# Prompt attention with packed score passes, plain float32 P v in column tiles, and row sums on VectorE and GpSimd

## Chip, core and metric

One core of one Trainium2 chip runs the kernel. The metric is the device time of one execution in microseconds (us). Three runs of the kernel before took 1915.83, 1916.79 and 1921.95 us; the median is 1916.79.

## What is computed

One hybrid decoder layer, for a prompt of 2048 tokens and 8 samples of 8 new tokens. A projection feeds a multi-head latent attention (MLA, 8 heads) and a gated linear attention (GLA, 4 heads); their outputs are gated, projected, and followed by a gated per-token term and a norm. The change lies in the prompt's MLA:

```
s = (einsum('bqhd,bkhd->bhqk', qn_b, k_nope)          # 64 values a head
     + einsum('bqhr,bkr->bhqk', qr_b, k_rope)) * scale  # 32 rotary values, one key for all heads
s = where(kpos <= qpos, s, -inf)
p = softmax(s)
o = einsum('bhqk,bkhd->bqhd', p, v)                   # 64 values a head
```

All of it is float32. TensorE's one-pass type, float32r, holds fewer bits, so the kernel splits operands in two float32r parts, hi + lo, and adds hi\*hi + hi\*lo + lo\*hi in PSUM.

## The kernel before

The work goes in stages: pass A (projections, queries, keys, values, stored to DRAM), pass B (GLA), prompt attention interleaved with the samples' decode attention, and the output projection. A scheduler that plays the program through puts the instructions of each engine in their final order; on each engine they run in that order.

`attention` is a generator. It goes over 32 units (h, j): 8 heads, and for each the query tiles j = 3, 2, 1, 0 of 512 queries. A unit has 4j + 4 key blocks of 128 keys, of which the last four lie on the diagonal and take only 512, 384, 256 and 128 queries (`c0`). For each block `attend` does this:

- three TensorE passes of float32r make the scores, keys on the partitions and queries along the row, in a PSUM tile `psC` of one bank, two in turn (L963 with the hi parts, 64 nope + 32 rope + 1 row for the maximum = 97 contraction rows; L964 and L965 with the lo parts, 96 rows);
- ScalarE takes the exponential twice, rounded (`ph`, L967) and full (`pf`, L969); VectorE makes `pl` = `pf` - `ph` (L971); on the diagonal GpSimd masks both (L974);
- three passes accumulate P v in `poC` (L976, L977, L978). The stationary side holds v's lo, hi and a block of ones, so that the row sums of P come out of the same passes.

Ahead of each unit `maxima` computes its row maxima: one score pass of the hi parts with queries on the partitions (L933) into `pmC`, reduced on VectorE (L935, L938, L940), transposed by L948 and copied by ScalarE into row 96 of the queries. The unit's loop mixes the next unit's maxima between its own blocks, and the main loop runs 0.8 attention steps for each step of `decode` (its TensorE passes are L770 to L833, its GpSimd work L51, L750 to L764). After a unit, `ob` is copied out and stored (L981 to L983).

The SBUF places of head 6's and 7's keys, values and queries are handed on to the output stage (`places`) for its weights; `early` is the place of head 6's values, through which the first weights are staged in three tiles.

Of the kernel before, what the change touches and what calls it, by code (L numbers as in the profile page):

```python
# [41 lines left out]
BASE = 8          # the innermost blocks of the GLA chunk  # L42
FLOOR = -20.0     # least log decay of a step inside them


def emit(ctx, tc, I, O):
# [48 lines left out]
    # hi and lo parts of queries, keys (both transposed) and values  # L95
# [3 lines left out]
    Kr = dram.tile([DR + 1, 2, S], F32, name="Kr")     # last row: ones  # L99
    Vd = dram.tile([NT, P, H, 2, DV], F32, name="Vd")  # L100
# [3 lines left out]
    Dd = dram.tile([H, S], F32, name="Dd")            # sums of P  # L104
    Rd = dram.tile([H, T], F32, name="Rd")            # their reciprocals
# [11 lines left out]
    # sample group, kept for the decode attention  # L117
# [19 lines left out]
    # ------------------------------------------------------------------ pass A: latents, queries, keys, values  # L137
    def pass_a(wb):
        """returns the weights of pass B, which take the place of this pass's as soon as these are done"""
        with ExitStack() as c:  # L140
# [17 lines left out]
            def xload(t0, W, add):  # L158
                """x^T in two parts, and the sums of squares over each partition's rows"""
# [22 lines left out]
            def scales(acc, W, tiles):  # L182
                """1 / rms of the tokens, along the rows (R) and along the columns"""
# [18 lines left out]
            def load_wide(ws, src, g=None, cp=A):  # L202
                """weights of each 128 rows of src, and of all its columns, into [P, hi|lo, columns] of ws"""
# [46 lines left out]
            def latents(z, q, i, m, lat, la, cs):  # L250
# [33 lines left out]
                # forget gate logits, from the low-rank rows and the row of ones  # L284
# [7 lines left out]
            def forget(la, W, t0):  # L292
                """log sigmoid(x) / 16, with log sigmoid(x) = min(x, 0) - ln(1 + exp(-|x|))"""
# [25 lines left out]
            def gates_sample(x, i, m, t0):  # L319
                """few tokens: they are the stationary side, and the result is transposed"""  # L320
# [41 lines left out]
            def keys_values(lat, t0, n):  # L362
# [8 lines left out]
                for q in range(n):  # L371
# [3 lines left out]
                    qq = sp.tile([P, H, 2, DV], F32R, name="qq", bufs=3)  # L375
                    zv = z.rearrange("p (h d) -> p h d", h=H)
                    split(qq[:, :, 1], qq[:, :, 0], zv)
                    nc.sync.dma_start(Vd[t0 // P + q], qq.bitcast(F32))

            for mi, (t0, W, tiles) in enumerate(macros):  # L380
# [29 lines left out]
                else:  # L410
                    # most of the gates last: their operands' places go to the weights of pass B as they are done
# [8 lines left out]
    def weights_b(ww, xp, gm):  # L420
        """in the places of pass A's operands, in the order in which it gives them up"""
# [13 lines left out]
    # ------------------------------------------------------------------ pass B: gated linear attention  # L435
    def pass_b(ws, xp, wb):
        with ExitStack() as c:
# [22 lines left out]
            rst = wp.tile([P, 4, P], F32, name="rst")       # 0 where a cumulation begins, else 1  # L460
# [10 lines left out]
            # second factors [2 heads x 64, pair, head of the pair, token], zero off the diagonal  # L471
# [4 lines left out]
            # state [2 heads x 64, pair, head of the pair, 128], zero off the diagonal  # L476
# [27 lines left out]
            def gla(cnt, i, m, qk, v, gt):  # L504
# [6 lines left out]
                # transposed q, k [2 heads x 64, pair, token] and cumulated log decay  # L511
# [8 lines left out]
                # inside the base blocks a step's log decay is held at -20 (e^-20 is far below a float32's last bit)  # L520
# [23 lines left out]
                # q exp(b), k exp(b_last - b)  # L544
# [13 lines left out]
                # A^T[s, t] by levels: first halves of blocks of 2L against their second halves  # L558
# [59 lines left out]
                # outputs and state  # L618
# [55 lines left out]
                # norm and gate  # L674
# [23 lines left out]
    # ------------------------------------------------------------------ decode attention  # L698
    def decode(c):
        """a generator; each step is a piece of work"""  # L700
# [5 lines left out]
        CK = 8                      # key blocks of 128 in a chunk  # L706
        NCK = 4                     # chunks of a sample
# [15 lines left out]
        # q in the latent space [c, b, hi|lo, h, t], and the rope stack [hi; hi; lo]  # L723
# [12 lines left out]
        qrs = wp.tile([96, NB, 2, H, TD], F32R, name="qrs")    # second half zero: it adds nothing to the lo rows  # L736
# [76 lines left out]
        def fresh(b, mx, dn, oc):  # L813
            """the keys of the new tokens"""
# [74 lines left out]
    # ------------------------------------------------------------------ prompt attention  # L889
    def attention(c, we, slots):  # L890
        """a generator; each step is a block of 128 keys against a tile of 512 queries.
        The places of the keys and values go to slots as they are done."""
# [4 lines left out]
        pS = pool(c, "psC", 2, PSUM, side="right")  # L897
# [5 lines left out]
        VT = [wp.tile([P, NT, 192], F32R, name=f"VT{i}") for i in range(2)]  # L903
        for k in KT:
            for a in range(4):
                nc.sync.dma_start(k[a][DN:97].bitcast(F32), Kr[:, :, a * 512:a * 512 + 512])
        for v in VT:
            gcopy(v[:, :, P:192], ones[:, 0:DV].unsqueeze(1).broadcast_to([P, NT, DV]))

        def load(h):  # L910
            k, v = KT[h % 2], VT[h % 2]
            for a in range(3, -1, -1):
# [367 lines left out]
```

## Time and profile before

| | |
|---|---|
| runs | 1915.83, 1916.79, 1921.95 us |
| profiled execution, first to last instruction | 1922.2 us |
| TensorE matmuls busy in it | 1786.5 us (93%) |
| VectorE, ScalarE, GpSimd busy | 1215.8, 919.9, 687.2 us |
| mean granted TensorE clock | 0.965 |

The profiled execution's span is 0.3% above the median of the runs. A matmul's row gives its shape as contraction rows\*stationary columns, then the moving operand. Matmuls overlap in the pipeline, so the time that a pass costs is read from one start to the next, not from the duration. A plain float32 matmul shows as two rows (x2), since it is carried out in two halves.

### The profile page before, as it was taken

The page shows a single profiled execution, that of the slowest core. Times are in us where ns is not written, and L with a number is a line of the kernel's source. Part 1 is how long each engine was busy: PE and PEld are TensorE (multiplying, and loading weights), DVE is VectorE, ACT ScalarE, POOL GpSimd, SP SyncE. Part 2 cuts the span into 40 slices and gives each one's busy share as a digit, 9 for nine tenths or more (in the row PEclk, how much of TensorE's full clock was granted, in tenths as well). Part 3 has the DMA queues.
Part 4 walks back from the last instruction along what each step waited for, and adds up shares of the span by engine and source line. Part 5 has one row for each costly group of instructions (what it writes and reads, how often), then busy time and mean ns, then how long its engine had stood idle before and what let it go on. Part 6 is the DMA issues. An engine that isn't in the chain of part 4 may idle for free.

```text
span 1922.2 us, 27335 instructions
## 1 busy us (share of the span) xinstructions
PE 1786.5 (93%) x9296; PEld 1427.9 (74%) x9296; DVE 1215.8 (63%) x2640; ACT 919.9 (48%) x2184; POOL 687.2 (36%) x1043
## 2 busy tenths in 40 slices
PE   4999987899999996999999999999998999999997
PEld 3877776688787784677777777777776788888885
DVE  6376466566744766788878888888887433323333
ACT  4354455334332433677776777777783112212112
POOL 5263352343433332544444444454436100000000
PEclk7999999899989997899999999999999999999999
DMA  5164476511111107223323232322217432222211
GB/s 167 42 232 158 147 267 212 136 39 38 48 31 45 45 23 178 68 71 94 83 78 100 58 86 72 97 80 77 79 37 237 120 94 83 88 84 73 77 48 33
DMA packets 150374, 183.74 MB, mean 96 GB/s; under 512 B 18682, under 2 KB 93291, under 8 KB 150235
## 3 DMA queue, kind: packets, MB, share of 16 engines
q1 hardware_dynamic: 144090, 161.02, 27.8%
q0 software_dynamic: 6144, 20.98, 3.6%
q8 instruction: 74, 1.21, 0.3%
q14 instruction: 66, 0.53, 0.1%
HBM read 125.60 MB, written 56.35 MB: 95 GB/s over the span
## 4 chain that ended last, share of the span: by engine, by line
PE 67%; DVE 5%; DMA 4%; ACT 2%; issue 1%; POOL 1%; SPq 0%; POOLq 0%; DVEq 0%; ACTq 0%
PE pgE L63 6%; PE pgE L65 6%; PE pgE L64 6%; PE pgB L65 4%; PE pgB L63 4%; PE pgB L64 4%; PE poC L976 3%; PE poC L978 3%; PE psC L963 3%; PE pmC L933 3%; PE poC L977 3%; PE psC L964 3%; PE psC L965 3%; DVE pl L971 1%; PE poD L803 1%
## 5 line engine op out<-in xcount | busy, mean ns | idle before, releaser
L971 DVE TENSOR_TENSOR pl<-pf,ph 128x512 fp32r<-128x512 f32 (+1 forms) x320 | 230.2, 724 | 42.4 <-ACT pf L969 38.2
L967 ACT ACTIVATE ph<-psC 128x512 fp32r<-128x512 f32 (+1 forms) x320 | 171.0, 534 | 126.2 <-PE psC L965 68.6
L969 ACT ACTIVATE pf<-psC 128x512 f32<-128x512 f32 (+1 forms) x320 | 170.2, 532 | 0.0
L935 DVE TENSOR_REDUCE mxC<-pmC 128x1 f32<-128x512 f32 x192 | 129.6, 682 | 30.4 <-PE pmC L933 28.3
L933 PE MATMUL pmC<-KT,qC 96*128 96x512 f32 (+2 forms) x320 | 122.8, 402 | 20.1 <-DVE mxC L940 6.5
L976 PE MATMUL poC<-ph,VT 128*128 128x512 f32 (+1 forms) x320 | 124.0, 387 | 4.5 <-ACT ob L981 3.0
L978 PE MATMUL poC<-pl,VT 128*128 128x512 f32 (+1 forms) x320 | 122.6, 384 | 2.0 <-DVE pl L971 1.8
L963 PE MATMUL psC<-qC,KT 97*128 97x512 f32 (+1 forms) x320 | 121.8, 381 | 0.5 <-ACT pf L969 0.4
L964 PE MATMUL psC<-qC,KT 96*128 96x512 f32 (+1 forms) x320 | 119.0, 372 | 0.0
L965 PE MATMUL psC<-qC,KT 96*128 96x512 f32 (+1 forms) x320 | 118.6, 371 | 0.0
L977 PE MATMUL poC<-ph,VT 128*64 128x512 f32 (+1 forms) x320 | 117.0, 366 | 0.0
L1146 ACT ACTIVATE thE<-pgE 128x512 f32<-128x512 f32 x32 | 19.1, 598 | 153.6 <-PE pgE L65 153.6
L1147 DVE SCALAR_TENSOR_TENSOR thE<-thE,pgE 128x512 f32<-128x512 f32 x32 | 22.0, 688 | 111.0 <-ACT thE L1146 111.0
L933 PEld LDWEIGHTS pmC<-KT,qC 96*128 96x128 f32 x320 | 62.4, 198 | 37.9 <-DVE mxC L935 10.9
L64 PE MATMUL pgE<-wpg,hh 128*128 128x512 f32 x224 | 87.7, 391 | 0.0
L63 PE MATMUL pgE<-wpg,hh 128*128 128x512 f32 x224 | 87.6, 391 | 0.0
L51 POOL TENSOR_SCALAR chl<-cr 128x1024 fp32r<-128x1024 f32 x32 | 38.3, 1198 | 137.4 <-PE poD L803 137.3
L65 PE MATMUL pgE<-wpg,hl 128*128 128x512 f32 x224 | 85.4, 392 | 0.0
L1150 POOL TENSOR_TENSOR ssE<-ssE 128x1 f32<-128x1 f32 (+1 forms) x17 | 3.3, 195 | 219.9 <-ACT yE L1149 219.9
L1090 POOL TENSOR_TENSOR raw<-raw 128x512 f32<-128x512 f32 (+1 forms) x17 | 22.2, 1308 | 161.5 <-DMA raw<-Rd 161.5
L60 DVE TENSOR_TENSOR x<-x 128x512 fp32r<-128x512 f32 (+2 forms) x74 | 64.5, 917 | 22.3 <-PE pgB L64 14.2
L750 POOL DMA_INDIRECT cr<-in_ckv,idx x32 | 36.7, 1148 | 116.5 <-PE poC L978 53.1
(475 smaller groups left out, 5396.3 us busy)
## 6 DMA issues: line engine op xcount, KB each, us to landing
x<-in_xT SPq DMA_DIRECT2D x32, 512.0 KB
x<-in_w_in SPq DMA_DIRECT2D x16, 512.0 KB
Qn<-qq SPq DMA_DIRECT2D x16, 512.0 KB
Kn<-qq SPq DMA_DIRECT2D x16, 512.0 KB
Vd<-qq SPq DMA_DIRECT2D x16, 512.0 KB
KT<-Kn SPq DMA_DIRECT2D x32, 256.0 KB
VT<-Vd SPq DMA_DIRECT2D x8, 1024.0 KB
qC<-Qn SPq DMA_DIRECT2D x32, 256.0 KB
```

What stands on the lines that cost most here:

```text
L63: T_.matmul(out, ah, bh, start=first, stop=False)
L64: T_.matmul(out, ah, bl, start=False, stop=False)
L65: T_.matmul(out, al, bh, start=False, stop=last)
L933: T_.matmul(ps[:, :w], qs, kv[0][cb][:96, 0, :w], start=True, stop=True)
L963: T_.matmul(ps[:, c0:], kh[:, ks], qh[:, c0:], start=True, stop=False)
L964: T_.matmul(ps[:, c0:], kh[:96, ks], ql[:, c0:], start=False, stop=False)
L965: T_.matmul(ps[:, c0:], kl[:, ks], qh[:96, c0:], start=False, stop=True)
L967: A.activation(ph[:, c0:], ps[:, c0:], AF.Exp, scale=SC)
L971: V.tensor_tensor(pl[:, c0:], pf[:, c0:], ph[:, c0:].bitcast(F32), op=ALU.subtract)
L976: T_.matmul(o[:, c0:], vt[:, kb, DV:192], ph[:, c0:], start=kb == 0, stop=False)
L977: T_.matmul(o[:DV, c0:], vt[:, kb, 0:DV], ph[:, c0:], start=False, stop=False)
L978: T_.matmul(o[:, c0:], vt[:, kb, DV:192], pl[:, c0:], start=False, stop=kb == nk - 1)
```

## The change

- **Scores.** The contraction of hi and lo parts, 3 x 96 rows and the maximum, is laid out in 2.5 passes of 128 rows. Pass 0 (l = 0, L980) holds 64 hi nope rows and the rope keys' hi and lo parts against the rope queries' hi; pass 1 (l = 1) holds nope lo\*hi and hi\*lo. What is left, rope hi against query lo and the row of ones for the maximum, are 33 rows: L983 takes them for an even block from partitions 0 to 32 and for the odd block from 64 to 96, two row tiles of 64. Keys and queries are loaded in more pieces (`load`, `queries`: 9 and 7 DMAs where 5 and 2 were), and pass A no longer splits v.
- **Blocks go in pairs.** One `psC` tile of two banks holds a pair's scores, and there is one such tile where there were two of one bank. Off the diagonal one exponential goes over both banks; its result `p` is plain float32.
- **P v.** L998 multiplies v (64 columns, float32, unsplit) with `p`; even blocks go to PSUM partitions 0 to 63, odd ones to 64 to 127. `ob` adds the halves (a ScalarE copy, a VectorE addition).
- **Sums.** `sum0` and `sum1` collect P along the keys: blocks with kb % 3 = 1 on VectorE, the others on GpSimd (L1007). After a unit L1017 sums over the partitions with a matrix of ones, 8 matmuls in column tiles of 32.
- **Places.** `early` has one staging tile where it had three; the list of places is rearranged.

```diff
-                T_.matmul(ps[:, c0:], kh[:, ks], qh[:, c0:], start=True, stop=False)
-                T_.matmul(ps[:, c0:], kh[:96, ks], ql[:, c0:], start=False, stop=False)
-                T_.matmul(ps[:, c0:], kl[:, ks], qh[:96, c0:], start=False, stop=True)
-                ph = pp.tile([P, 512], F32R, name="ph")
-                A.activation(ph[:, c0:], ps[:, c0:], AF.Exp, scale=SC)
-                pf = pp.tile([P, 512], F32, name="pf")
-                A.activation(pf[:, c0:], ps[:, c0:], AF.Exp, scale=SC)
...
-                T_.matmul(o[:, c0:], vt[:, kb, DV:192], ph[:, c0:], start=kb == 0, stop=False)
-                T_.matmul(o[:DV, c0:], vt[:, kb, 0:DV], ph[:, c0:], start=False, stop=False)
-                T_.matmul(o[:, c0:], vt[:, kb, DV:192], pl[:, c0:], start=False, stop=kb == nk - 1)
+        pS = pool(c, "psC", 1, PSUM, side="right")
...
+            for k0 in range(0, nk, 2):
+                pair = [(kb, kb % 2, max(kb - 4 * j, 0) * P) for kb in (k0, k0 + 1)]
+                ps = pS.tile([P, 2, 512], F32, name="psC")
+                for kb, e, c0 in pair:
+                    ks = slice(kb % 4 * P, kb % 4 * P + P)
+                    for l in range(2):
+                        T_.matmul(ps[:, e, c0:], kt[kb // 4][:, l, ks], q[:, l, c0:], start=l == 0, stop=False)
+                for kb, e, c0 in pair:
+                    rows = slice(64 * e, 64 * e + 33)
+                    T_.matmul(ps[:, e, c0:], K3[rows, kb // 2], q[rows, 2, c0:], start=False, stop=True)
+                yield
+                p = pp.tile([P, 2, 512], F32, name="p")
+                if k0 < 4 * j:
+                    A.activation(p, ps, AF.Exp, scale=SC)
+                else:
+                    for kb, e, c0 in pair:
+                        A.activation(p[:, e, c0:], ps[:, e, c0:], AF.Exp, scale=SC)
+                        G.affine_select(p[:, e, c0:c0 + P], p[:, e, c0:c0 + P], pattern=[[1, P]],
+                                        compare_op=ALU.is_ge, fill=0.0, base=0, channel_multiplier=-1)
...
+                for kb, e, c0 in pair:
+                    T_.matmul(o[64 * e:64 * e + 64, c0:], vt[:, kb], p[:, e, c0:], start=kb < 2, stop=kb >= nk - 2)
+                for kb, e, c0 in pair:
+                    f = kb % 3 == 1
...
+                        (V if f else G).tensor_tensor(sums[f][:, c0:], sums[f][:, c0:], p[:, e, c0:], op=ALU.add)
+                yield
...
+            for e in range(2):
+                for i in range(4):
+                    T_.matmul(sm[32 * i:32 * i + 32, :P], ones[:, :32], sums[e][:, i * P:(i + 1) * P], start=e == 0, stop=e == 1)
```

The built order shows where this puts the instructions. TensorE before, in the middle of the attention; L963 to L965 are a block's scores, L976 to L978 its P v, L933 a pass of the next unit's maxima, L770 to L783 the decode attention:

```order
L963 MATMUL psC<-qC,KT_6778 128x512
L964 MATMUL psC<-qC,KT_6778 128x512
L965 MATMUL psC<-qC,KT_6778 128x512
L781 MATMUL ptD<-cth,qlat 128x512
L782 MATMUL ptD<-ctl,qlat 64x512
L783 MATMUL ptD<-krT,qrs 128x512
L770 MATMUL ptD<-ident,cr 128x128 x4
L963 MATMUL psC<-qC,KT_6778 128x512
L964 MATMUL psC<-qC,KT_6778 128x512
L965 MATMUL psC<-qC,KT_6778 128x512
```

Two blocks' scores can stand there in a row, since there are two tiles for them. TensorE now, with two pairs of blocks off the diagonal (L980 and L983 scores, L998 P v, L949 maxima; the numbers of the decode's lines are lower by two):

```order
L998 MATMUL poC<-p,VT_6766 64x512 x2
L980 MATMUL psC<-qC,KT_6758 128x512 x4
L983 MATMUL psC<-qC,K_6765 128x512 x2
L774 MATMUL ptD<-identr,krs 96x128 x4
L949 MATMUL pmC<-KT_6758,qC 128x512
L779 MATMUL ptD<-cth,qlat 128x512
L780 MATMUL ptD<-ctl,qlat 64x512
L998 MATMUL poC<-p,VT_6766 64x512 x2
```

Each pair's P v follows its scores with maxima and decode work in between, and the next pair's scores follow P v. At a unit's end, on the diagonal, TensorE's order now is:

```order
L998 MATMUL poC<-p,VT_6767 64x512
L774 MATMUL ptD<-identr,krs 96x128 x4
L998 MATMUL poC<-p,VT_6767 64x384
L779 MATMUL ptD<-cth,qlat 128x512
L780 MATMUL ptD<-ctl,qlat 64x512
L980 MATMUL psC<-qC,KT_6761 128x512 x4
L983 MATMUL psC<-qC,K_6765 128x512 x2
L1017 MATMUL pmC<-sum_13379,ones 32x128
L949 MATMUL pmC<-KT_6761,qC 128x128
L998 MATMUL poC<-p,VT_6767 64x256
```

The two P v matmuls of a pair stand apart there, with other passes between them.

More of the change, by code (lines that the diff above doesn't have):

```diff
@@ L923, in maxima @@
+            for l in range(2):
+                nc.sync.dma_start(qf[0:DN, l], Qn[hs, 0, ts])
+            nc.sync.dma_start(qf[DN:P, 1], Qn[hs, 1, ts])
+            for r0 in (64, 96):
+                nc.sync.dma_start(qf[r0:r0 + DR, 0], Qr[rs, 0, ts])
+            for r0 in (0, 64):
+                nc.sync.dma_start(qf[r0:r0 + DR, 2], Qr[rs, 1, ts])
+            return q
         def maxima(j, kv, q):
@@ L948, in maxima @@
                 T_.matmul(mr[0:1, i * P:(i + 1) * P], m4r[:, i:i + 1], identr, start=True, stop=True)
-            A.activation(qh[96:97], mr[0:1], AF.Copy)
+            for r0 in (32, 96):
+                A.activation(q[r0:r0 + 1, 2], mr[0:1], AF.Copy)
             yield
         def attend(h, j, kv, q):
-            (kt, vt), qt = kv, q
-            qh, ql = qt[:, 0], qt[:96, 1]
+            kt, vt = kv
             o = po.tile([P, 512], F32, name="poC")
+            sums = [sp.tile([P, 512], F32, name=f"sum{e}") for e in range(2)]
@@ new lines, in attend @@
+            ob = sp.tile([DV, 512], F32, name="ob")
+            A.activation(ob, o[DV:P], AF.Copy)
+            V.tensor_tensor(ob, ob, o[:DV], op=ALU.add)
+            nc.sync.dma_start(Od[h * DV:(h + 1) * DV, j * 512:j * 512 + 512], ob)
+            sm = pm.tile([P, 512], F32, name="pmC")
+            for e in range(2):
+                for i in range(4):
+                    T_.matmul(sm[32 * i:32 * i + 32, :P], ones[:, :32], sums[e][:, i * P:(i + 1) * P], start=e == 0, stop=e == 1)
+            rc = sp.tile([P, P], F32, name="rcC")
```

110 lines of the change are left out of this document (51 added, 59 removed).

## Prediction

> **What bounds the kernel now.** I read the page's first part, then the windows, to see which engine limits the stage that is changed.
>
> ```profile
> span 1922.2 us, 27335 instructions
> PE 1786.5 (93%) x9296; PEld 1427.9 (74%) x9296; DVE 1215.8 (63%) x2640; ACT 919.9 (48%) x2184; POOL 687.2 (36%) x1043
> ...
> core 0: us, PE busy (x) PEld busy (x) DVE busy (x) ACT busy (x) POOL busy (x), PEclk, DMA share, GB/s
> 900.00:1000.00 100.00, 96.48 (x556) 76.83 (x555) 85.27 (x225) 77.90 (x163) 51.29 (x76) 1.00 0.31 85
> 1100.00:1200.00 100.00, 94.84 (x527) 75.15 (x527) 85.01 (x223) 74.40 (x160) 45.13 (x69) 0.98 0.30 83
> ```
>
> The attention is TensorE's: it is busy 95 to 96 of 100 us, at the full clock. VectorE (85) and ScalarE (75 to 78) are near, GpSimd (45 to 51) is not. The stage's length is in the first and last starts of its maxima and of its last P v pass:
>
> ```profile
> L933 PE MATMUL pmC<-KT,qC x320: 220/394/796, 752.7 to 1434.4; 96*128 96x512 f32 x128, 96*128 96x128 f32 x16, 96*128 96x384 f32 x16
> L978 PE MATMUL poC<-pl,VT x320: 224/394/793, 792.0 to 1459.3; 128*128 128x512 f32 x128, 128*128 128x256 f32 x32
> ```
>
> That is 707 us, 752.7 to 1459.3. So the price of a TensorE pass decides. The timeline gives it from start to start, and the groups by form the number of passes:
>
> ```profile
> 1304.00 0.40 PE L933 MATMUL pmC<-KT,qC 96*128 96x512 f32 x1
> 1304.23 0.40 PE L963 MATMUL psC<-qC,KT 97*128 97x512 f32 x1
> ...
> 1305.18 0.39 PE L976 MATMUL poC<-ph,VT 128*128 128x512 f32 x1
> 1305.41 0.40 PE L977 MATMUL poC<-ph,VT 128*64 128x512 f32 x1
> 1305.64 0.40 PE L963 MATMUL psC<-qC,KT 97*128 97x512 f32 x1
> ...
> L976 PE MATMUL poC<-ph,VT 128*128 128x512 f32 x224 | 94.3, 421 | 4.5 <-ACT ob L981 3.0 <-POOL ph L974 1.4
> L976 PE MATMUL poC<-ph,VT 128*128 128x384 f32 x32 | 11.7, 366 | 0.0
> L976 PE MATMUL poC<-ph,VT 128*128 128x256 f32 x32 | 10.1, 316 | 0.0
> L976 PE MATMUL poC<-ph,VT 128*128 128x128 f32 x32 | 7.8, 243 | 0.0
> ```
>
> A 512-wide pass costs 0.235 us (seven in 1.64). Each kind of pass has 224 x 512 + 32 x (384 + 256 + 128) = 139,264 columns, as much as 272 full passes or 136 full pairs of blocks.
>
> **Packing: what it saves on TensorE.** For plain float32 in tiled modes, pass B has two places to read. In the first, single matmuls (x2 rows) in two different tilings alternate; in the second, four matmuls go to two column tiles in turn, between full-array passes:
>
> ```profile
> 569.66 0.43 PE L657 MATMUL poB<-ident,oi 128*64 128x128 f32 x2
> 570.02 0.43 PE L656 MATMUL poB<-v,AT 64*64 64x128 f32 x2
> 570.38 0.43 PE L657 MATMUL poB<-ident,oi 128*64 128x128 f32 x2
> ...
> 577.19 0.39 PE L63 MATMUL pgB<-wg,x 128*128 128x512 f32 x1
> 577.42 0.39 PE L64 MATMUL pgB<-wg,x 128*128 128x512 f32 x1
> 577.74 0.65 PE L666 MATMUL ptB<-v,km 64*64 64x128 f32 x8
> 578.32 0.50 PE L65 MATMUL pgB<-wg,x 128*128 128x512 f32 x1
> 578.66 0.40 PE L63 MATMUL pgB<-x 128*128 128x512 f32 x1
> ```
>
> Call w a 128-column float32 matmul, s a change of tiling. The first place gives w + s = 0.36. The second gives 0.58 for four matmuls and one change: with two at a time, 2w + s = 0.58. So w = 0.22 and s = 0.14. One at a time, 4w + s = 0.58 would leave w = 0.07, less than one 128-column pass of float32r at full rate for what must be several (0.235 / 4 = 0.06). So column tiles do run together. As a check on s over the whole visit: from 577.42 to 578.66 are 1.24 us, in which two full passes (0.46) and 2w (0.44) account for 0.90; 0.34 is left for going in and out, 0.17 each. I take 0.15 for a change.
>
> A full pair of blocks took 12 passes, 2.82 us. Now it takes five (the two L983 row tiles counted as one), 1.18, and P v with 512 columns at 4w = 0.88, together 2.06. It saves 0.76, and over 136 pairs 104 us. Three things take from that:
>
> - On the diagonal the pair's halves are of unequal width, and the tiles last as long as the wider; and 34 of the 160 pairs have their two L998 apart in the built order (the third piece of order above), so that each pays alone. Added up over the order with w, P v comes to 141 us instead of 136 x 0.88 = 120: 21 lost. L983 loses 2.
> - The sums, L1017: 8 matmuls a unit in four column tiles, 8w / 4 = 0.44, over 32 units 14; many stand apart, so 18.
>
> Net, 104 - 41 = 63 us less work.
>
> **Packing: what it costs.** Counted in the built orders from the first maxima to the last pass of the attention, TensorE changes its tiling 115 times before and 851 times now: full array to row tiles (L983), back to maxima or decode, to column tiles (L998), back again. That is 736 more, at 0.15 us 110 us. The Trainium skill, page "TensorEngine Tiling (Array Packing)", section "Tiling Modes", speaks against the change here: it says that changing the tiling mode, not merely the tile, drains TensorE. The trace agrees where rows or float32 column tiles change (0.14 to 0.17 us), but not for the 64-column float32r pass L977, which stands between full passes at the usual 0.23 us.
>
> Sum for TensorE: -63 + 110 = +47 us.
>
> **The other engines and the waits.** They get lighter or stay covered:
>
> ```profile
> L967 ACT ACTIVATE ph<-psC 128x512 fp32r<-128x512 f32 x224 | 134.1, 599 | 107.0 <-PE psC L965 60.8 <-PE poC L977 26.6 <-PE pmC L933 8.2
> L967 ACT ACTIVATE ph<-psC 128x256 fp32r<-128x256 f32 x32 | 12.3, 385 | 0.8 <-PE psC L965 0.2
> L971 DVE TENSOR_TENSOR pl<-pf,ph 128x512 fp32r<-128x512 f32 x224 | 161.4, 725 | 35.4 <-ACT pf L969 33.3 <-PE poC L978 0.6
> L764 POOL TENSOR_TENSOR chl<-cr,chl 128x1024 fp32r<-128x1024 f32 x32 | 77.7, 2429 | 1.3
> ```
>
> ScalarE: by the two widths an exponential costs 0.17 us and 0.84 ns a column, so 1.03 for two banks where four of 0.60 were: some 185 us less. VectorE loses the subtractions and gains 72 additions of about 0.7 us, copies and reciprocals: some 120 less. GpSimd gains 184 additions; at 2.43 us for 1024 columns a 512-wide one is 1.2, together 220 us, less 64 masks' worth; it goes from about 330 to 520 busy of 750 us. It stays under TensorE.
>
> The new wait is the single `psC` tile: a pair's P v and the next pair's scores both wait for its exponential. From the start of the last score pass that is 0.40 (its duration) + 1.03 + about 0.1, and 1.3 us of it are free for other passes. In the order stand there maxima and decode passes, 1.24 us in the median by the spacings above; what is missing to 1.3 adds up to 31 us over the 160 pairs. Queued behind the waiting L998 are the next scores and the maxima; ScalarE and VectorE wait for those. Against it stand the waits that were named before:
>
> ```profile
> PE pmC L948 <- DVE mxC L927: 7.0, 10, 0.8
> PE pmC L933 <- DVE mxC L940: 6.5, 6, 1.4
> ...
> PE pmC L933 <- DVE mxC L935: 3.3, 6, 1.2
> PE poC L976 <- ACT ob L981: 3.0, 7, 1.0
> ```
>
> About 20 us that lighter engines may end, and as much again, since a pass after a wait starts with an unhidden weight load. I set the two against each other, 0, with -45 and +80 as bounds: everything named gone twice over; or the 31 us paid and another 50 where the diagonal's P v waits for masks that stand behind additions on GpSimd (64 diagonal pairs, up to one 1.2 us addition each, less what is covered).
>
> **Other stages.** Pass A's values lose a split, of which TensorE's wait may give back some:
>
> ```profile
> L63 PE MATMUL pq<-lat,wq 128*128 128x512 f32 x48 | 19.3, 427 | 13.4 <-DVE qq L60 11.5 <-DVE th L350 1.9
> ...
> 1456.36 4.57 DMA yE<-in_w_out
> ```
>
> At most 11, I take 5. The output's first weights go through one staging tile instead of three; if one load (4.57 us) falls behind the attention's end, it costs 5. Together 0. The extra DMAs lie under a DMA share of 0.3.
>
> **The sum.** 1922.2 + 47 = 1969 us on the profiled execution, whose span is 0.3% over the median: 1963 us.
>
> **Rivals.**
>
> 1. *The changes of tiling hide in waits: faster.* TensorE waits for the exponential in many pairs anyway, and a drain there costs nothing. The decision is at 63 / 0.15 = 420 paid changes of the 736; if half are paid (55 us) and the lighter engines give 25, it is 1963 - 55 - 25 = 1883 us. For it: 1.24 us of cover against 1.3. Against: only changes next to P v's wait can hide, at most about one in four. Chance 0.2.
> 2. *The loop over one score tile decides.* Scores, exponential and P v of a pair in turn, and masks behind additions on GpSimd: +80, 2043 us. For it: TensorE's order leaves P v directly behind the exponential, and 34 split pairs. Against: the median cover. Chance 0.2.
> 3. *Column tiles at 512 columns do not run together.* Then P v takes 2 x 0.88 a pair, +120: 2080 us. Against: L666. The Trainium skill, page "TensorE: Matmul & The Clock Gate", part "Packing small matmuls", gives 2.38 times for three column tiles of 512 columns, not 3; an estimate by that ratio puts 30 us on my sum. Chance 0.06.
>
> **How the numbers follow.** My forecast, about 1963 (1935 to 1995), gets 0.54. The range takes the bounds of the waits: 1963 - 45, and 18 more for a sixth of the changes hidden, is 1900; 1963 + 82 is 2045. A measurement of this kernel can tell about 0.3%, 6 us, from no change. Below 1911: rival 1 and a little of the forecast's lower tail, 0.2; within, 0.07; slower, 0.73.
>
> **What would show it.** Right: pairs of L998 start within 0.02 us of each other and last 0.86 to 0.9; 0.3 instead of 0.23 us ahead of each L983 and L998 and some 0.1 more behind; a stage of about 750 us in place of 707, with ScalarE under 55% and VectorE under 70% busy. Wrong: passes around L983 at 0.23 us (no drain for float32r row tiles); L998 halves one after the other; or waits of L998 on ScalarE and GpSimd of over 100 us.

## The result and the profile after

The changed kernel takes 2039.22 us, the median of four runs (2035.97 to 2042.3), where the kernel before takes 1916.31 on the same chip (1913.7 to 1921.95): 1.0635 times as long, 95% interval 1.0615 to 1.0656. The prediction had 1963 us.

The page after, and its windows at the two places that were read before:

```profile
span 2038.1 us, 27357 instructions
PE 1878.9 (92%) x9488; PEld 1314.0 (64%) x9488; DVE 1144.6 (56%) x2461; ACT 797.6 (39%) x1800; POOL 854.8 (42%) x1137
```

```profile
core 0: us, PE busy (x) PEld busy (x) DVE busy (x) ACT busy (x) POOL busy (x), PEclk, DMA share, GB/s
900.00:1000.00 100.00, 95.42 (x517) 52.49 (x515) 68.07 (x174) 55.21 (x100) 70.14 (x83) 0.97 0.35 92
1100.00:1200.00 100.00, 93.86 (x508) 51.99 (x508) 67.04 (x176) 52.69 (x95) 66.97 (x79) 0.97 0.32 86
1480.00:1500.00 20.00, 14.14 (x55) 6.61 (x55) 14.92 (x34) 3.44 (x7) 4.78 (x11) 0.71 0.38 107
```

VectorE and ScalarE are as light as foreseen, GpSimd as heavy; TensorE still looks 94 to 95% busy. Busy time alone does not show what it is busy with. The first and last starts of the maxima and of P v give the stage's length again:

```profile
L949 PE MATMUL pmC<-KT,qC x320: 218/470/796, 751.7 to 1567.0; 128*128 128x512 f32 x128, 128*128 128x128 f32 x16, 128*128 128x384 f32 x16
L998 PE MATMUL poC<-p,VT x640: 272/592/1116, 785.7 to 1580.3; 128*64 128x512 f32 x128, 128*64 128x256 f32 x32
```

Before, the stage ran from 752.7 to 1459.3. Now it begins at 751.7, and from the last P v start at 1580.3 it goes on to the last sums: 832 us against 707. All of the 123 us lie there. The timeline shows what a visit to a tiling costs; each row's first number is its start, and what counts is the distance to the next start:

```profile
1203.62 1.08 PE L998 MATMUL poC<-p,VT 128*64 128x512 f32 x4
1204.63 1.19 PE L980 MATMUL psC<-qC,KT 128*128 128x512 f32 x4
1205.76 0.49 PE L983 MATMUL psC<-qC,K 33*128 33x512 f32 x2
1206.18 0.50 PE L779 MATMUL ptD<-cth,qlat 128*128 128x512 f32 x1
1206.52 0.39 PE L780 MATMUL ptD<-ctl,qlat 128*64 128x512 f32 x1
1206.74 0.40 PE L781 MATMUL ptD<-krT,qrs 96*128 96x512 f32 x1
1207.07 0.71 PE L795 MATMUL ptD<-ident,sc 64*128 64x64 f32 x8
```

Four score passes take 1.13 us where four at 0.235 are 0.94: about 0.1 is lost behind P v and as much ahead of L983. The two row tiles L983 take 0.42 where one pass takes 0.235, so leaving them costs 0.19. The full pass behind (L779) takes 0.34 instead of 0.23, another 0.1. L780, a 64-column float32r pass among full ones, costs nothing extra, as before. So a visit to the row tiles costs about 0.39 us, two changes. P v of a full pair takes 1.01 from its start to that of the next pass; in the records its two halves start 7 ns apart.

With these allowances each spacing of TensorE's matmuls in the stage can be put down to streaming, to a change of tiling (the excess on the change and on the pass behind it, up to 0.1 us each, 0.2 out of L983) or to waiting (all the rest, slower passes at half clock included). This is my own sum over all the records, in us:

| stage | length | streaming | changes of tiling (count) | waiting | at half clock |
|---|---|---|---|---|---|
| before | 707 | 583 | 18 (113) | 106 | 55 |
| after | 832 | 531 | 148 (849) | 153 | 105 |
| difference | +125 | -52 | +130 (736) | +47 | +50 |

The split depends on the allowances, by some 5 us. The last column is the time in which the trace shows a granted clock of 0.5; part of it is also counted as waiting. Passes that start in such stretches hold 54 us of the waiting now and 30 before; if each of them is given at most its own length again for its slowness, that is 28 us now and 16 before. So half clock alone explains at most some 12 of the +47. TensorE's waits are still not long by name (the row of L71 is pass A's):

```profile
PE pmC L949 <- DVE mxC L951: 14.0, 24, 1.3
PE poC L998 <- POOL p L992: 12.8, 13, 3.6
PE pg L71 <- ACT w L133: 9.0, 1, 9.0
PE poC L998 <- ACT p L987: 6.1, 9, 1.2
```

By the spacings 48 us are lost ahead of L949 (30 ahead of its counterpart before), 28 ahead of L998 (26 ahead of P v before), 12 ahead of L980 (13 ahead of the scores before) and 48 ahead of the decode's passes (23 before). So the growth stands ahead of the maxima and the decode, and not ahead of P v or the scores.

### The profile page after: what moved, and what is told of

Read it like the earlier page. It is cut to its first block, busy times and chain, and to the rows that moved or that the text cites. A ratio compares the mean times of both kernels' runs of the same rounds, so it can differ in the third digit from the quotient of the medians.

```text
span 2038.1 us, 27357 instructions
## 1 busy us (share of the span) xinstructions
PE 1878.9 (92%) x9488; PEld 1314.0 (64%) x9488; DVE 1144.6 (56%) x2461; ACT 797.6 (39%) x1800; POOL 854.8 (42%) x1137
## 4 chain that ended last, share of the span: by engine, by line
PE 66%; DVE 8%; POOL 3%; ACT 3%; DMA 2%; issue 2%; SPq 0%; POOLq 0%; ACTq 0%; DVEq 0%
PE poC L998 7%; PE pgE L63 7%; PE pgE L64 7%; PE pgE L65 7%; PE psC L980 6%; PE pgB L64 4%; PE pgB L63 4%; PE pgB L65 4%; PE pmC L949 3%; PE psC L983 2%; PE pmC L1017 1%; DVE mxC L951 1%; PE ptD L768 1%; PE poD L801 1%; POOL sum L1007 1%
## 5 line engine op out<-in xcount | busy, mean ns | idle before, releaser
L1007 POOL TENSOR_TENSOR sum<-sum,p 128x512 f32<-128x512 f32 (+3 forms) x184 | 206.2, 1121 | 104.0 <-ACT p L987 99.3
L998 PE MATMUL poC<-p,VT 128*64 128x512 f32 (+3 forms) x640 | 184.2, 569 | 20.2 <-POOL p L992 12.8
L980 PE MATMUL psC<-qC,KT 128*128 128x512 f32 (+3 forms) x640 | 173.9, 393 | 2.6 <-ACT p L990 2.3
L980 PEld LDWEIGHTS psC<-qC,KT 128*128 128x128 f32 x640 | 106.9, 192 | 105.5 <-issue 77.5
L987 ACT ACTIVATE p<-psC 128x1024 f32<-128x1024 f32 x96 | 98.3, 1024 | 184.8 <-PE psC L983 148.9
L949 PE MATMUL pmC<-KT,qC 128*128 128x512 f32 (+2 forms) x320 | 138.4, 468 | 26.5 <-DVE mxC L951 14.0
L949 PEld LDWEIGHTS pmC<-KT,qC 128*128 128x128 f32 x320 | 60.3, 201 | 82.5 <-DVE mxC L951 30.7
L1007 DVE TENSOR_TENSOR sum<-sum,p 128x512 f32<-128x512 f32 (+3 forms) x72 | 72.3, 1005 | 42.9 <-POOL p L992 25.3
L998 PEld LDWEIGHTS poC<-p,VT 128*64 128x64 f32 x640 | 41.4, 137 | 69.2 <-POOL p L992 19.0
L983 PE MATMUL psC<-qC,K 33*128 33x512 f32 (+1 forms) x320 | 81.7, 471 | 0.6 <-ACT qC L966 0.4
L60 DVE TENSOR_TENSOR x<-x 128x512 fp32r<-128x512 f32 (+2 forms) x74 | 64.9, 917 | 29.6 <-PE pgB L64 20.2
L762 POOL TENSOR_TENSOR chl<-cr,chl 128x1024 fp32r<-128x1024 f32 x32 | 76.6, 2393 | 1.3
```

Of the source, the lines that this page charges most:

```text
L60: V.tensor_tensor(lo, src, hi.bitcast(F32), op=ALU.subtract)
L762: G.tensor_tensor(chl[:, 1], cr, chl[:, 0].bitcast(F32), op=ALU.subtract)
L949: T_.matmul(ps[:, :w], qs, kv[0][cb][:, 0, :w], start=True, stop=True)
L980: T_.matmul(ps[:, e, c0:], kt[kb // 4][:, l, ks], q[:, l, c0:], start=l == 0, stop=False)
L983: T_.matmul(ps[:, e, c0:], K3[rows, kb // 2], q[rows, 2, c0:], start=False, stop=True)
L987: A.activation(p, ps, AF.Exp, scale=SC)
```

## The experiments

The medians and ratios below stand each against runs of the kernel before on the same chip (1917 to 1920 us). The columns are those of the table above, from each kernel's own trace. Some edits also change which SBUF places the output stage gets for its weights; that lies outside the stage's columns:

| kernel | us | ratio, 95% interval | stage | streaming | changes (count) | waiting | half clock |
|---|---|---|---|---|---|---|---|
| after | 2039 | 1.0635, 1.0615-1.0656 | 832 | 531 | 148 (849) | 153 | 105 |
| rope scores as full passes | 2034 | 1.0607, 1.0565-1.0648 | 828 | 557 | 89 (558) | 182 | 128 |
| row tiles apart | 2151 | 1.1204, 1.1150-1.1257 | 946 | 562 | 209 (1160) | 176 | 206 |
| P v as full passes | 2184 | 1.1394, 1.1344-1.1444 | 958 | 518 | 111 (587) | 329 | 298 |
| decode slowed | 2122 | 1.1073, 1.1028-1.1119 | 804 | 504 | 143 (810) | 157 | 123 |
| scores first | 2011 | 1.0461, 1.0423-1.0499 | 805 | 527 | 134 (776) | 144 | 147 |
| scores first, rope full | 1989 | 1.0366, 1.0327-1.0404 | 784 | 558 | 91 (574) | 135 | 98 |
| exponential twice | 2208 | 1.1522, 1.1425-1.1619 | 1005 | 527 | 147 (824) | 331 | 347 |
| no sums | 1997 | 1.0409, 1.0365-1.0452 | 789 | 522 | 142 (805) | 125 | 109 |
| scores first, rope full, no sums | 1952 | 1.0182, 1.0159-1.0206 | 739 | 551 | 86 (538) | 102 | 69 |
| two-pass P v on the kernel before | 2130 | 1.1106, 1.1059-1.1152 | 900 | 530 | 19 (114) | 351 | 319 |
| the same, no sums | 1946 | 1.0155, 1.0131-1.0178 | 723 | 529 | 18 (114) | 176 | 115 |
| mask as a pass, on the kernel before | 1933 | 1.0094, 1.0071-1.0117 | 722 | 591 | 18 (114) | 113 | 65 |

### Are the changes of tiling the cost?

The first four kernels weigh two theories, as each text has them: A, the changes of tiling are paid in full; B, the loop over the one score tile and its waits decide, and changes are largely hidden in it.

**Rope scores as full passes.** The row tiles go; the second key tile and the queries get zero rows, so that L983 is two full-array passes.

```
...
-T_.matmul(ps[:, e, c0:], K3[rows, kb // 2], q[rows, 2, c0:], start=False, stop=True)
+T_.matmul(ps[:, e, c0:], K3[e][:, kb // 2], q[:, 2, c0:], start=False, stop=True)
```

> L983 goes over all 128 rows (a second key tile holds zeros where the other block's rows lie), so that it needs no row tiles; a pair's two passes come one after the other. In the built order the changes of tiling go from 851 to 559 and TensorE's work rises by 23 us. Theory A, each change costs TensorE about 0.18 us whatever else waits: 292 x 0.18 = 52 us less, 23 more, so about 29 us faster than the changed kernel, near 2010. Theory B, the changes lie beside waits for the exponential, GpSimd and the clock, and those make the loss: 23 us slower, near 2062.

Measured 2034 us, which is neither (2010 or 2062). The changes fell by 59 us as A has it and streaming rose by 26, but 29 came back as waiting.

**Row tiles apart.** Each block's L983 stands right behind its own two L980, so that the two no longer share a visit.

```
-                for kb, e, c0 in pair:
                     rows = slice(64 * e, 64 * e + 33)
                     T_.matmul(ps[:, e, c0:], K3[rows, kb // 2], q[rows, 2, c0:], start=False, stop=True)
```

> Each block's L983 is issued directly behind its own two L980, so that the two row tiles of a pair stand apart. Changes of tiling go from 851 to 1162, TensorE's work rises by 29 us. Theory A: 311 x 0.18 + 29 = 85 us slower than the changed kernel, near 2124. Theory B, changes are mostly hidden: at most the 29 us, 2039 to 2068.

2151 us, on A's side and 27 over it. 311 more changes cost 60 us by the spacings, 0.19 each; 31 more us of streaming, since the two row tiles no longer run together, and 23 of waiting make up the rest. Adding changes is paid in full; taking them away was not.

**P v as full passes.** Two float32r passes of [v hi, v lo] over two parts of P; the second exponential and VectorE's subtraction return.

```
-T_.matmul(o[64 * e:64 * e + 64, c0:], vt[:, kb], p[:, e, c0:], start=kb < 2, stop=kb >= nk - 2)
+T_.matmul(o[:, c0:], vt[:, kb], ph[:, e, c0:], start=kb == 0, stop=False)
+T_.matmul(o[:, c0:], vt[:, kb], pl[e][:, c0:], start=False, stop=kb == nk - 1)
```

> P v goes back to float32r, as two full-array passes a block (v's hi and lo side by side, 128 columns, against P's hi and then P's lo); the second exponential and VectorE's subtraction are back. Changes of tiling go from 851 to 589, TensorE's work falls by 12 us. Theory A: 262 x 0.18 + 12 = 59 us faster than the changed kernel, near 1980, up to 2010 if VectorE becomes the bound. Theory B, waits make the loss: ScalarE and VectorE get some 300 us of work back, so no faster than 2030.

2184 us, B. Streaming and changes fell by 50 us together, waiting rose by 176. The loop over the one score tile had become longer by an exponential and a subtraction, and the subtraction took 1062 ns in its 512-wide form beside the additions of the sums, where it took 725 in the kernel before. How much of the 176 is the longer loop and how much the slow subtraction was not separated.

**Decode slowed.** By the built order 408 of the attention's 1856 matmuls come after the decode's last, against 9 of 2240 before; the decode's passes are what fills TensorE's waits. Here its chunk buffers are one instead of two, so that it reaches further.

```
-        cp = pool(c, "cD", 2)
+        cp = pool(c, "cD", 1)
```

> The decode attention's gathered pages have one buffer instead of two, which slows its own chain, so that its passes last to the attention's end (in the changed kernel 408 of the attention's 1856 matmuls come after the last of them). Changes of tiling 810 instead of 851. Theory A: 7 us from the changes, and of the 42 us of waits after the decode's end perhaps half: 10 to 30 us faster than the changed kernel. Theory B, the cover that runs out is the main loss: 45 us or more faster, under 1995. If decode work spills into the output stage, some of either is lost.

2122 us. The stage's waiting stayed (157), and the decode ran on behind the attention. In the stage's last 157 us, which hold no decode pass in the changed kernel, TensorE loses 42 us there and 27 here; what was saved came back elsewhere (the named waits of L964 went from 3.4 to 13.0 us). So the end of the filler is at most some 15 us of the waits, not the main part of them.

### Does the loop decide?

From here on the theories are L (the loop) and T (TensorE's own work and its changes).

**Scores first.** The next pair's scores are issued ahead of this pair's P v, which then need not stand right behind its exponential.

```
...
+                if k0 + 2 < nk:
+                    nxt = scores(k0 + 2)
+                    yield
                 for kb, e, c0 in pair:
                     T_.matmul(o[64 * e:64 * e + 64, c0:], vt[:, kb], p[:, e, c0:], start=kb < 2, stop=kb >= nk - 2)
```

> The changed kernel with one thing moved: the next pair's scores are issued ahead of this pair's P v, so that the P v of a pair lies beside the exponential of the next and no longer waits right behind its own. Instructions and work are the same; counted in the built order the attention stage has 778 changes of TensorE's tiling instead of 849 and some 4 us less of streaming. Theory L (the loop scores, exponential, P v over the one two-bank score tile decides together with TensorE's order; the 153 us in which TensorE waits in the stage are that loop's): the waits fall by some 45 to 65 us and the time by these and the 13 us of the changes: 1960 to 1985 us, half clock in the stage well under 105 us. Theory T (the time is TensorE's own work and 0.18 us for each change of tiling; the waits are VectorE's, GpSimd's and the decode's and stay): only the 71 changes and the streaming, 15 us less: 2015 to 2030 us.

2011 us, between the two and nearer to T. The group of P v passes shows that its own wait went. It had 20.2 us of idle time in the changed kernel:

```profile
L998 PE MATMUL poC<-p,VT 128*64 128x512 f32 (+3 forms) x640 | 184.2, 569 | 20.2 <-POOL p L992 12.8
```

and with scores first:

```profile
L1006 PE MATMUL poC<-p,VT 128*64 128x512 f32 (+3 forms) x640 | 181.1, 573 | 2.8 <-POOL p L997 2.1
```

But the waiting in all fell by only 9 us, with 147 us at half clock; of the 27 us of the stage 14 are changes of tiling. L had promised 45 to 65 us of waits. The order is a part of the waiting, and by this run a small one.

**Scores first, rope full.** The first kernel's edit and the order together.

> The same order of scores and P v together with the rope scores as full-array passes with zero rows (no row tiles). Counted in the built order: 576 changes of tiling in the attention stage instead of 849, 27 us more of streaming. Theory L: the changes saved are no longer given back as waits of the loop: 2039 - 273 x 0.178 + 27 - some 50 of waits = 1955 to 1980 us, and 10 us or more under the kernel with the order alone. Theory T: 2039 - 49 + 27 = 2017 us, or the 2034 us of the rope scores in full passes in the old order, less 15: 2010 to 2030.

1989 us, between the two. The full rope passes, worth 5 us (within the intervals) in the old order, are worth 22 in this one: the changes are 43 us less, streaming 31 more, waiting 9 less. In the old order what they saved came back as waiting; here it did not.

**Exponential twice.** The same values written twice; ScalarE alone gets 98 us more.

```
-                    A.activation(p, ps, AF.Exp, scale=SC)
+                    for _ in range(2):
+                        A.activation(p, ps, AF.Exp, scale=SC)
```

> The changed kernel with the exponential of each full pair issued twice, the second over the first with the same values: nothing is added on TensorE, VectorE or GpSimd, and ScalarE, 39% busy, gets 96 times 1.02 us, 98 us in all. Only the loop over the score tile grows longer, by 1.02 us a turn. Theory L: most of it lands on the time: 2110 to 2150 us. Theory T: ScalarE has the room and the work in between covers it: under 2065 us.

2208 us: 169 us for 98 us of work on an engine that is 39% busy, more than L had. Here T is wrong, and L right in kind. The longest wait by name is the loop's, P v for the exponential; 347 us of the stage are at half clock:

```profile
PE poC L999 <- ACT p L988: 37.9, 22, 3.2
PE pmC L949 <- DVE mxC L951: 18.7, 36, 2.3
```

So the loop has no slack; but taking the order's share of it away does not bring the time back.

### The sums on VectorE and GpSimd

**No sums.** The additions L1007 go, and nothing else.

```
-                    else:
-                        (V if f else G).tensor_tensor(sums[f][:, c0:], sums[f][:, c0:], p[:, e, c0:], op=ALU.add)
```

> The changed kernel without the additions of the row sums (L1007): 206 us of GpSimd and 72 us of VectorE are left out, and the output is divided by the first two blocks' sums alone. TensorE's work is the same; counted in the built order there are 805 changes of tiling instead of 849. Theory H (the additions hold up what TensorE waits for: the maxima's reductions on VectorE, 48 us of waits before L949, and the masks on GpSimd, 13 us before L998): the waits before L949 fall to the 30 us that the kernel before has, those on the masks go, and the half clock with them: 1985 to 2005 us. Theory T (the waits come of TensorE's own order and the one score tile, the additions are beside it): only the 44 changes, 8 us, and the streaming's 4: 2020 to 2035 us.

1997 us, in H's range: work that TensorE does not do costs 42 us. The waiting fell by 28 us, ahead of L949 from 48 to 34, near the 30 of the kernel before; changes and streaming by 15. The half clock, which H had going too, stayed at 109 us. The groups of the changed kernel show that a 512-wide addition is dearer than I had it (1.2 us on GpSimd, 0.7 on VectorE):

```profile
L1007 POOL TENSOR_TENSOR sum<-sum,p 128x512 f32<-128x512 f32 x120 | 159.5, 1329 | 102.6 <-ACT p L987 99.3 <-ACT pn L59 0.6 <-DVE mxC L956 0.2
L1007 DVE TENSOR_TENSOR sum<-sum,p 128x512 f32<-128x512 f32 x48 | 49.1, 1024 | 23.0 <-ACT p L987 17.5 <-POOL p L992 5.4
```

**All three together.** Scores first, rope full, no sums.

> Three edits together on the changed kernel: scores ahead of P v, the rope scores as full-array passes, and no additions of the row sums (the output is divided by the first two blocks' sums alone). Apart they gave 2039 - 1989 = 50 us (the first two) and 2039 - 1997 = 42 us (the third). Theory Add (each removes costs of its own: the order and the row tiles on one side, the engines' additions on the other): 1935 to 1960 us; what is left over the kernel before is then the 540 changes of tiling against 115, 425 x 0.16 = 68 us, less the streaming saved. Theory Same (both remove the same waits, the ones in front of P v): 1975 to 1990 us.

1952 us, as Add has it. The sum closes: the waiting is 102 us, where the kernel before has 106. What is left over the kernel before in the stage, 32 us, is 68 us of changes less 31 of streaming, and -4 of waiting. The 102 are not the same waits, though: by the spacings 6 us stand ahead of P v (26 before) and 40 ahead of the decode's passes (23 before). That the totals agree is in part chance.

### Without changes of tiling

**Two-pass P v on the kernel before.** Scores stay in three full passes over two score tiles; one of three P v passes goes, the row sums go to GpSimd, and the mask is added on TensorE.

```
-                T_.matmul(o[:, c0:], vt[:, kb, DV:192], ph[:, c0:], start=kb == 0, stop=False)
-                T_.matmul(o[:DV, c0:], vt[:, kb, 0:DV], ph[:, c0:], start=False, stop=False)
-                T_.matmul(o[:, c0:], vt[:, kb, DV:192], pl[:, c0:], start=False, stop=kb == nk - 1)
+                T_.matmul(o[:, c0:], vt[:, kb], ph[:, c0:], start=kb == 0, stop=False)
+                T_.matmul(o[:, c0:], vt[:, kb], pl[:, c0:], start=False, stop=kb == nk - 1)
...
+                    G.tensor_tensor(sums[:, c0:], sums[:, c0:], pf[:, c0:], op=ALU.add)
```

> Built on the kernel before: the scores stay as three full-array float32r passes over two one-bank score tiles, P v becomes two full-array float32r passes (v's leading and trailing parts side by side in 128 columns, against P's two parts) instead of three, the row sums are added up on GpSimd and summed by four one-column matmuls a unit, and the mask is added to the scores by a 128-column pass instead of GpSimd's selects. Counted in the built order: 116 changes of tiling against 115 of the kernel before, 48 us less of TensorE's streaming. VectorE's work is the same (85% busy in that stage), GpSimd gets some 300 us of additions less 83 us of selects, 85 to 90% of the stage. Theory T (time is TensorE's streaming plus 0.18 us a change of tiling, and a saving without changes of tiling stays saved): 1917 - 48, a little of it given back: 1865 to 1885 us. Theory W (work taken off TensorE turns into waits for the other engines, changes of tiling or not): 1900 to 1940 us.

2130 us, worse than W had it. VectorE's subtraction (`pl`) had been 725 ns in its 512-wide form; with GpSimd's additions beside it:

```profile
L972 DVE TENSOR_TENSOR pl<-pf,ph 128x512 fp32r<-128x512 f32 x224 | 238.0, 1068 | 35.9 <-ACT pf L970 34.2 <-PE poC L974 1.3
L933 DVE TENSOR_REDUCE mxC<-pmC 128x1 f32<-128x512 f32 x192 | 129.2, 681 | 36.5 <-PE pmC L931 36.1
```

The maxima's reduction, which reads PSUM, keeps its 681 ns (682 before). TensorE waits for the late subtraction (31.6 us by name, its longest wait), and the stage has 319 us at half clock.

**The same, no sums.** Only the additions go.

> The kernel with P v in two full-array passes, without GpSimd's additions of the row sums (L978, 383 us): the output is divided by the first block's sums alone. Everything else stays. Theory V (GpSimd's additions slow VectorE, whose subtraction takes 994 ns beside them and 724 in the kernel before, and with VectorE late TensorE waits and falls into half clock for 345 us): the subtraction returns to 700 to 740 ns, half clock to under 100 us, and the time to 1860 to 1890 us, since TensorE streams some 50 us less than before and changes its tiling as rarely. Theory R (the two-pass P v or the mask's pass is itself what costs, whatever the additions do): over 1990 us, half clock over 200 us.

1946 us. The additions had cost 184 us, and the subtraction returns, nearly as V has it:

```profile
L972 DVE TENSOR_TENSOR pl<-pf,ph 128x512 fp32r<-128x512 f32 x224 | 170.3, 762 | 35.1 <-ACT pf L970 30.4 <-PE poC L974 2.6 <-ACT s2D L784 0.6
```

But V's 1860 to 1890 us fails: the kernel is still 1.3 to 1.8% slower than before. Of its 29 us, 16 lie in the stage. Streaming is 54 us less and the changes are as few as before, but 70 us more stand under waiting. 30 of them are no wait: they are the sums' one-column matmuls, 0.11 us apart, which my sum had put at almost nothing. So 24 us less of work on TensorE came with 40 us more of waiting. Of these, 12 are two waits for a DMA. The output stage's first transposes (L1092) stand inside the attention in this order, and their data had not landed; in the kernel before they stand at its end and wait for nothing in the stage:

```profile
1439.81 0.90 PE L1092 MATMUL ptE<-ident,raw 128*128 128x128 f32 x3 [4.49 <-DMA raw<-MGd]
1454.64 1.11 PE L1092 MATMUL ptE<-ident,raw 128*128 128x128 f32 x4 [7.49 <-DMA raw<-MGd]
```

What the other 28 wait for was not tried further and stays open.

**Mask as a pass, on the kernel before.** GpSimd's selects against a 128-column pass.

```
+                if dg >= 0:
+                    T_.matmul(ps[:, c0:c0 + P], cmr, identr, start=False, stop=True)
...
-                    for x in (ph, pl):          # keys after the query
-                        G.affine_select(x[:, c0:c0 + P], x[:, c0:c0 + P].bitcast(F32), pattern=[[1, P]],
```

> The kernel before with one edit: the mask is added to the scores by a 128-column pass of TensorE, and GpSimd's 256 selects (83 us) behind the two parts of P go. TensorE gets 128 passes of 0.075 us, 10 us. Theory V (what GpSimd does beside VectorE and in front of P v costs more than the same work on TensorE): 1895 to 1912 us, VectorE's subtraction under 724 ns. Theory T (TensorE's streaming sets the time): 1925 to 1930 us.

1933 us, 0.7 to 1.2% slower, T and a little more. V fails in the time. The selects do slow the subtractions that they stand beside, on the diagonal, as the 384-wide ones show in the kernel before and in this one:

```profile
L971 DVE TENSOR_TENSOR pl<-pf,ph 128x384 fp32r<-128x384 f32 x32 | 30.5, 952 | 4.8 <-ACT pf L969 4.3
L974 DVE TENSOR_TENSOR pl<-pf,ph 128x384 fp32r<-128x384 f32 x32 | 19.0, 593 | 6.4 <-ACT pf L972 6.4
```

But most subtractions are 512 wide, and these got no faster (771 ns against 725), so that nothing came of it. No version tried is faster than the kernel before.

## Why the prediction was wrong

The direction was right, but the move was +123 us where +46 was forecast. 2039 us lies outside the forecast's own 1935 to 1995, and inside the wide range of 1900 to 2045 only by luck: the upper end stands for 80 us of waits for the exponential and the masks, ahead of P v and the scores, and there TensorE loses 40 us where it lost 39 before. In the stage +125 stood against a sum of +47; 78 us are to be explained.

1. **The waits, set to 0: the step that failed.** They are +47. The prediction set "the single `psC` tile" and its 31 us against 20 us of named waits "that lighter engines may end", twice over. Nothing of those ended: ahead of the maxima TensorE waits 48 us instead of 30, since VectorE, lighter in all, has additions of 1.02 us between its reductions. Leaving the additions out takes 28 us of waiting off: that part is shown. The rest went only with three edits together (102 against 106 before), and the order alone took 9; which of the order and the row tiles it hangs on, and why 48 us instead of 23 stand ahead of the decode's passes, stays open. Half clock alone, whose stretches grew from 55 to 105 us, is at most some 12 of the 47.
2. **The price of a change, 0.15 us: too low.** It is 0.18 in the mean (130 us over 736), +20. For P v it was right: 0.1 ahead, 0.1 behind, 0.15 in the visit (a pair takes 1.01 us up to the next pass, and two pairs without a pass between them 1.87, so a pair streams in 0.86). The float32r row tiles L983 cost more, 0.39 us a visit. My two places of pass B had row and column tiles of plain float32 alone. The mechanism and the count (736 in the order, 736 in the trace) were right.
3. **The saving, 63 us: a little too high.** 52, +11. P v streams in 142 us, as the prediction had it (141). The sums L1017 take 23 instead of 18, L983 some 2 more, and the passes that went 3 less; the rest is spread. That column tiles run together was right, but one step to it was not: the 0.07 us left for a float32 matmul one at a time is not less than a float32r pass of 0.06, only too close to it.
4. **The other engines.** ScalarE at 53 to 55% and VectorE at 67 to 68% are what was named. But "They get lighter or stay covered" drew from shares what has to be drawn from queues. GpSimd's and VectorE's additions were costed as if each ran alone, at 1.2 and 0.7 us; they took 1.33 and 1.02, and 42 us of the time. (The masks fell from 256 to 128, by 128 and not by 64; for GpSimd's load that is 21 us.)
5. **Rival 1** (changes hide in waits) is out: 311 added changes cost 0.19 us each and more. Something of it holds the other way round: removing 291 changes in the old order saved 5 us in all, since waits took their place.
6. **Rival 2** (the loop over one score tile, +80, 2043 us) has the time but not the account: in the place of its 80 stand 47 of waits, 20 of dearer changes and 11 of streaming, and the waits did not grow ahead of P v and the scores, where it has them. That the loop has no slack is shown, though: 1.02 us more in each of 96 turns costs 169 us. **Rival 3** is out: the two 512-wide matmuls of a pair take 1.01 us up to the next pass, and one that stands alone takes 1.00.

What would have shown me wrong was badly chosen. I named over 100 us of waits of L998 on ScalarE and GpSimd; 19 are there by name and 28 by the spacings, as many as before; the growth lies ahead of L949 and the decode's passes.

The opening claim, that "the price of a TensorE pass decides", holds for passes that are added (the mask, the row tiles apart). For work that goes it was not borne out: 24 us less of it without more changes of tiling, and with the sums left out, did not make the kernel before faster, though 12 us of what came in its place are a DMA that was late.

## What to carry to other kernels

Packing small matmuls saves array time and pays for each visit: count the visits in the built order, and set them at the spacing that the trace shows for that very kind of tile, both ways. Where three engines are 75 to 95% busy and meet in one in-order loop, take no saving on one of them as time until you have asked what the loop waits for next; work moved from the bounding engine to others is not free because they had idle time, above all if these hold each other up. A test that lengthens the loop on an idle engine (here the exponential twice) is cheap and shows at once whether there is slack.

## What the runs showed of the hardware

- **VectorE and GpSimd hold each other up.** A 512-wide subtraction of two SBUF operands takes 725 ns on VectorE in the kernel before, 1068 beside GpSimd's additions, 762 without them; a reduction out of PSUM stays at 681. The Trainium skill, page "SBUF — State Buffer", section "Who interferes with whom", says that a VectorE instruction with two SBUF inputs contends with a GpSimd instruction that reads SBUF, and that a reduction never does on this chip; both runs agree.
- **Leaving float32r row tiles costs 0.19 us on top of the pass behind them**, where entering a tiling costs 0.09 and the first full pass after one 0.1. The Trainium skill, page "TensorEngine Tiling (Array Packing)", section "Tiling Modes", says only that a change of mode drains TensorE; the trace agrees that each change costs time, and gives it these prices. The weight loads (PEld) show where a part of it lies. L779, the first full pass behind L983, and L983 itself start together with their own weight load; L780, which follows without a change, had its load 0.23 us ahead of it:

```profile
1205.76 0.19 PEld L983 LDWEIGHTS psC<-qC,K 33*128 33x128 f32 x2 [0.36 <-issue]
1206.18 0.19 PEld L779 LDWEIGHTS ptD<-cth,qlat 128*128 128x128 f32 x1 [0.24 <-issue]
1206.29 0.14 PEld L780 LDWEIGHTS ptD<-ctl,qlat 128*64 128x64 f32 x1
```

In the kernel before, a 512-wide pass behind a wait starts with its load in the same way and takes 0.33 us up to the next (median of 26) instead of 0.235. So the 0.1 us on the first pass behind a change is as much as a weight load that is not hidden costs.

- **Half clock comes with short waits, not only with long ones.** From 1487 to 1495 us of the changed kernel, near the attention's end, TensorE has one or two passes between waits for VectorE (in brackets: its idle time before them):

```profile
1487.26 0.97 PE L949 MATMUL pmC<-KT,qC 128*128 128x512 f32 x2 [0.80 <-DVE mxC L951]
1488.54 1.28 PE L949 MATMUL pmC<-KT,qC 128*128 128x512 f32 x2 [0.31 <-DVE mxC L951]
1490.12 1.40 PE L949 MATMUL pmC<-KT,qC 128*128 128x512 f32 x2 [0.30 <-DVE mxC L951]
1492.82 0.80 PE L949 MATMUL pmC<-KT,qC 128*128 128x512 f32 x1 [1.30 <-DVE mxC L951]
1494.02 0.80 PE L949 MATMUL pmC<-KT,qC 128*128 128x512 f32 x1 [0.40 <-DVE mxC L951]
```

The single passes last 0.80 us instead of 0.40; the granted clock from 1480 to 1500 is 0.71. Half-clock stretches in the trace last 3.4 us or multiples of it, 17 us here. With the exponential twice, the half clock grew from 105 to 347 us as 98 us of work became 169; passes that start in it can hold 80 us more of the stage by their own slowness at most, counted as above. How much of the 169 that is was not separated.
